# A background of index scores and selection, paced at other rates

## The chip, the cores and the metric

The kernel runs on one core of one Trainium2 chip. A time is device microseconds of one execution; before the change the median of 3 runs is 3255.93 us (3255.27 to 3256.39). TensorE is called PE here, VectorE DVE, ScalarE ACT, GpSimd POOL, and SyncE, which issues most DMAs, SP.

## The reference

One residual block over 2048 rows of width 1024, in float32. What matters here is the indexer of the sparse attention, cut to its core:

```
proj = x @ w_in                       # q, latent, q_idx, w_idx, k_idx, pool_in, gate_logits
# rotary turn of q, k_lat, q_idx, k_idx
for each block of 128 queries:
    rel = relu(einsum('bqhd,bsd->bqhs', q_idx, k_idx) * idx_scale)        # 8 index heads
    score = einsum('bqh,bqhs->bqs', w_idx * head_w_scale, rel)            # inadmissible: -inf
    sel = top_k(score, 256)
    attention over the 256 kept keys (8 heads, shared latent key)
branch_b = multiscale_pool(pool_in) @ w_pool_branch
x = LN(alpha*x + (gate_a*(attn @ w_attn_branch) + gate_b*branch_b) @ w_out)
x = LN(alpha*x + conv_ffn(x))
```

## The kernel before

Every float32 matrix product is done as three products of split operands (`mm3`, line 308: high times high, high times low, low times high). A weight tile is split once, on POOL for the projections (`split`, line 293: a tensor_scalar, then a tensor_tensor that subtracts).

The 2048 rows are worked in four row groups of 512 (`run`, line 1851). First comes the index stage: `proj_index` for the groups 0 to 3 makes the index queries and keys. A second loop then runs `proj_pool`, `proj_q` and `proj_gates` for the groups 0 to 3. In its first round, group 0, the weights are loaded raw, split on POOL and stored; the rounds 1 to 3 load the split parts. Then follow the attention, the output projection and the FFN.

Beside this foreground runs a background: three generators (`GROUPS`, line 65), one for the row groups 0 and 1, one for group 2, one for group 3. Each first makes index scores (`index_scores`, line 879), then selects (`select`, line 946).

- A score step is one index head of one block, or of one half of the keys of a longer block: two or four matmuls, a Relu on ACT, and on DVE a scalar_tensor_tensor (`b<-b,ws,b`) that adds the weighted scores up. It ends in the bare `yield` at line 942. When a block is next in line its query rows are loaded by a DMA on SP (`m<-qi`), doubled on DVE, transposed on PE and split.
- The selection finds for every row the value of its 256th largest score bit by bit, 32 bits. A selection step counts one block against the candidate: DVE counts the front keys (a tensor_scalar that accumulates, `m,cd<-b,F`; the trace calls it TENSOR_SCALAR_CACHE_REDUCE, with a DVE_READ_ACCUMULATOR behind it), ACT the back keys (Sign, `m<-b,F`). After the blocks of a half three small DVE instructions decide the bit (`g<-cd,ca`, `h<-g`, `F<-h,F`); the next count of that half needs F. For the first generator a bit takes six steps (blocks 2, 3 and blocks 4 to 7).
- Then the equal values are counted (`m,c2<-b,F`), and for each block ACT makes signs (`b<-b,tn`), DVE a prefix sum and three more passes, and the mask goes to DRAM over SP.

What sets the order is a planner. `Clocks` and `Paced` (lines 86 to 135) add up an estimated time for each instruction of PE, DVE, ACT and POOL as the program is written. After each step of the foreground `turn` (line 329) adds to a credit the estimated PE time that has passed, times RATE, up to CAP. While credit is left and the estimated backlog of DVE or ACT is below SLACK, it takes the next background step and subtracts the larger of its estimated DVE and ACT time. So RATE is the share of estimated PE time that the background gets.

The attention of row group 3 needs the masks of the blocks 12 to 15. `load_masks` (line 1069) runs whatever is left of the background on the spot, ahead of all later attention work, when the first unit of that group is loaded.

Of the kernel before, what the change touches and what calls it, by code (L numbers as in the profile page):

```python
# [67 lines left out]
NFIRST = 1  # L68
FINE = "fine"
PAUSE = "pause"  # L70
GRAIN = 1
RATE = 0.75
CAP = 1.5
EARLY = 2
SWITCH = "A--"
# [169 lines left out]
class Kern:  # L245
    def __init__(self, ctx, tc, a, out):
        self.ctx = ctx
        self.clocks = Clocks()
        self.tc, self.nc, self.a, self.out = tc, PacedCore(tc.nc, self.clocks), a, out
        self.stores, self.older, self.bg, self.late = [], [], [], []  # L250
        self.const = ctx.enter_context(tc.tile_pool(name="const", bufs=1))
        self.big = ctx.enter_context(tc.tile_pool(name="big", bufs=42))
        self.mid = ctx.enter_context(tc.tile_pool(name="mid", bufs=8))
        self.sm = ctx.enter_context(tc.tile_pool(name="sm", bufs=4))
        self.p1 = ctx.enter_context(tc.tile_pool(name="p1", bufs=4, space=PSUM))
        self.p2 = ctx.enter_context(tc.tile_pool(name="p2", bufs=2, space=PSUM))
        self.early = ExitStack()
        self.keys_pool = self.early.enter_context(tc.tile_pool(name="keys", bufs=1))
        self.dram = ctx.enter_context(tc.tile_pool(name="dram", bufs=1, space=bass.MemoryType.DRAM))
        self.n = 0  # L260
        self.credit = self.seen = 0.0

    def _name(self, s):
        self.n += 1
        return f"{s}{self.n}"
# [63 lines left out]
    def turn(self, step=None):  # L329
        for t in self.late:  # L330
            t[0] -= 1
        while self.late and self.late[0][0] <= 0:
            self.late.pop(0)[1]()
        if step != FINE:
            for dst, src in self.older:
                self.nc.sync.dma_start(dst, src)
            self.older, self.stores = self.stores, []
        pe, work = self.clocks.pe, self.clocks.work
        self.credit = min(self.credit + RATE * (pe - self.seen), CAP)
        self.seen = pe  # L340
        while self.bg and self.clocks.backlog() < SLACK and self.credit > 0:
            ready, gen = self.bg[0]
            if not ready():
                break
            before = dict(work)
            step = next(gen, "end")
            if step == "end":
                self.bg.pop(0)
            if step == PAUSE:
                break  # L350
            self.credit -= max(work["dve"] - before["dve"], work["act"] - before["act"])

    def run_to_end(self, gen):
        for step in gen:
# [163 lines left out]
    def proj_t(self, ps, w, c0, pairs=range(DC // 2)):  # L518

        for dc in (2 * c + i for c in pairs for i in range(2)):  # L520
# [3 lines left out]
            self.mm3(ps, wh[:, j, c0:c0 + P], wl[:, j, c0:c0 + P], xh[:, i], xl[:, i], dc == 0, dc == DC - 1)  # L524
            if i and dc + 1 < DC and (dc // 2) % GRAIN == GRAIN - 1:
                yield FINE
# [352 lines left out]
    def index_scores(self, g):  # L879
        nc = self.nc  # L880
        blocks = [b for b in range(g * RB, (g + 1) * RB) if b >= 2]
        rows, doubled, parts = {}, {}, {}

        def load(b):
            rows[b] = self.M([P, IH * ID])
            nc.sync.dma_start(rows[b], self.d_qi[b])

        def double(b):
            qd = doubled[b] = self.T([P, IH, 2, ID])
            nc.vector.tensor_copy(qd, rows.pop(b).rearrange("p (h d) -> p h d", d=ID)[:, :, None, :]  # L890
                                  .to_broadcast([P, IH, 2, ID]))

        def prepare(b):
            qd = doubled.pop(b)
            ps = self.PS2([P, IH, P])
            for h in range(IH):
                nc.tensor.transpose(ps[:, h], qd[:, h].rearrange("p a d -> p (a d)"), self.ident)
            parts[b] = self.split_new(ps)

        load(blocks[0])  # L900
        for _ in range(PN[0] if g in PG else 1):
            yield PAUSE
        double(blocks[0])
        for _ in range(PN[1] if g in PG else 1):
            yield PAUSE
        prepare(blocks[0])
        for _ in range(PN[2] if g in PG else 1):
            yield PAUSE
        for b in blocks:
            N = P * (b + 1)  # L910
            more = b + 1 in blocks
            if more:
                load(b + 1)
            qh, ql = parts.pop(b)
            if N <= 1024:
                spans = [(0, N)]
            else:
                spans = [(0, N - SPLIT[b // 2]), (N - SPLIT[b // 2], N)]
            tiles = [self.T([P, hi - lo]) for lo, hi in spans]
            self.I[b] = tiles  # L920
            for h in range(IH):
                if h == HD and more:
                    double(b + 1)
                if h == HP and more:
                    prepare(b + 1)
                wsc = self.ws[:, b, h:h + 1]
                for t, (lo, hi) in enumerate(spans):
                    nch = 1 if hi - lo <= 512 else 2
                    cw = (hi - lo) // nch
                    ps = self.PS2([P, 2, 512])  # L930
                    for c in range(nch):
                        ks = slice(lo + c * cw, lo + c * cw + cw)
                        nc.tensor.matmul(ps[:, c, :cw], qh[:, h], self.kst[:, ks], start=True, stop=False)
                        nc.tensor.matmul(ps[:, c, :cw], ql[:, h], self.kst[:, ks], start=False, stop=True)
                    rl = self.T([P, nch, cw])
                    nc.scalar.activation(rl, ps[:, :nch, :cw], AF.Relu, scale=ID ** -0.5)
                    rl = rl.rearrange("p c w -> p (c w)")
                    if h == 0:
                        nc.vector.tensor_scalar(tiles[t], rl, wsc, None, op0=OP.mult)
                    else:  # L940
                        nc.vector.scalar_tensor_tensor(tiles[t], rl, wsc, tiles[t], op0=OP.mult, op1=OP.add)
                    yield
            w = tiles[-1].shape[1]
            getattr(nc, MS).memset(tiles[-1][0:64, w - 64:w], NEG)

# [905 lines left out]
    def run(self):  # L1851
# [23 lines left out]
            done = self.finish_index(g)  # L1875
        self.load_parts(0, range(NFIRST, DC // 2))
        for g in range(NG):
            for i, step in enumerate(self.proj_pool(g)):
                if i == 1 and g == 0:
                    done()  # L1880
                    self.wi_parts = None
                self.turn(step)
            self.run_to_end(self.proj_q(g))
            self.run_to_end(self.proj_gates(g))
# [40 lines left out]
```

## Time and profile before

| | us |
|---|---|
| median of 3 runs | 3255.93 |
| the profiled execution | 3255.52 |
| its span, first to last instruction | 3253.7 |
| PE busy | 3106.2 |
| DVE busy | 2415.8 |
| ACT busy | 1613.8 |
| POOL busy | 642.8 |

The span is 1.8 us short of the execution's own time. PE is busy 95% of it, so 147.5 us are left in which it does nothing. Busy time of PE also grows where its granted clock falls. In this trace the index stage runs to about 218 us, the first row group's projections from 218 to 437 us, those of the groups 1 to 3 to 1082 us, and the attention to 1588 us.

### The profile page before, as it was taken

Reading aid. Unit: us, or ns where it says so; the run is one execution under the profiler, and the core shown is the slowest. Engines: PE = TensorE matmul, PEld = TensorE weight load, DVE = VectorE, ACT = ScalarE, POOL = GpSimd, SP = SyncE. Lnnn points to the kernel's source line nnn. Section 1 sums busy time; section 2 is a strip of 40 time slices with the busy share of each in tenths; the row PEclk is TensorE's granted clock in tenths of the full one; section 3 lists DMA queues with packets and bytes.
Section 4 is the critical chain, followed back from the end, with each engine's and each line's share of the span. In section 5 each row is a group of like instructions: output and inputs, shape, how many; then the busy total and the mean of one; then the engine's idle time right before and its main releaser. Section 6 shows DMA issues by size and latency. Waiting matters only on the chain. (4 is left out here: it accounts for less than half of the span.)

```text
span 3253.7 us, 44390 instructions
## 1 busy us (share of the span) xinstructions
PE 3106.2 (95%) x15014; PEld 2585.8 (79%) x15014; DVE 2415.8 (74%) x4642; ACT 1613.8 (50%) x3068; POOL 642.8 (20%) x592
## 2 busy tenths in 40 slices
PE   8998899999999999699999999999999999999998
PEld 8886688888888787488787877878788887888876
DVE  5589987987799989988766799889855555453465
ACT  3365746874678777577411244444432232442343
POOL 2027410010010211000412244445111111000000
PEclk9999899999999999899999999999999999999999
DMA  7667784754575332211546788788666665653554
GB/s 250 233 203 275 247 329 160 259 213 166 177 265 205 118 105 62 93 59 62 200 143 208 262 281 297 285 298 295 245 213 217 225 228 199 234 197 109 205 222 154
DMA packets 306833, 666.88 MB, mean 205 GB/s; under 512 B 25322, under 2 KB 130222, under 8 KB 306606
## 3 DMA queue, kind: packets, MB, share of 16 engines
q1 hardware_dynamic: 297966, 648.31, 56.6%
q10 hardware_dynamic: 8640, 15.73, 1.3%
q8 instruction: 119, 1.95, 0.2%
q14 instruction: 108, 0.88, 0.1%
HBM read 434.67 MB, written 229.28 MB: 204 GB/s over the span
## 5 line engine op out<-in xcount | busy, mean ns | idle before, releaser
L133 PE MATMUL p<-b,b 128*128 128x512 f32 (+3 forms) x12832 | 2888.3, 381 | 104.6 <-ACT b L133 37.9
L133 PEld LDWEIGHTS p<-b,b 128*128 128x128 f32 x12832 | 2305.6, 190 | 559.4 <-ACT b L133 40.7
L133 ACT ACTIVATE b<-p 128x512 fp32r<-128x512 f32 (+11 forms) x618 | 351.5, 603 | 245.8 <-PE p L133 235.5
L133 DVE TENSOR_TENSOR b<-p,b 128x512 fp32r<-128x512 f32 (+5 forms) x574 | 362.7, 652 | 148.5 <-PE p L133 102.7
L133 ACT ACTIVATE b<-b 128x1024 fp32r<-128x1024 f32 (+2 forms) x310 | 265.8, 874 | 305.3 <-DVE b L133 94.0
L133 ACT ACTIVATE m<-b,F 128x448 bf16<-128x448 f32 (+3 forms) x448 | 366.3, 821 | 87.9 <-DVE F L133 69.3
L133 DVE TENSOR_SCALAR_CACHE_REDUCE m<-b,F 128x512 bf16<-128x512 f32 (+6 forms) x476 | 370.0, 808 | 0.9
L133 DVE TENSOR_TENSOR b<-b,b 128x1024 fp32r<-128x1024 f32 (+4 forms) x224 | 282.9, 1268 | 72.4 <-ACT b L133 48.3
L133 POOL TENSOR_TENSOR b<-b,b 128x1024 f32<-128x1024 f32 (+3 forms) x94 | 231.5, 2464 | 480.5 <-DVE b L133 399.0
L133 DVE SCALAR_TENSOR_TENSOR b<-b,cw,b 128x1022 f32<-128x1022 f32 (+1 forms) x176 | 248.0, 1419 | 94.4 <-ACT b L133 93.5
L133 ACT ACTIVATE b<-m 128x512 fp32r<-128x512 f32 (+1 forms) x248 | 143.9, 587 | 301.0 <-DVE m L133 121.4
L133 ACT ACTIVATE b<-b,cw 128x1024 f32<-128x1024 f32 x88 | 106.8, 1236 | 290.0 <-DVE b L133 290.0
L133 DVE TENSOR_TENSOR b<-m,b 128x512 fp32r<-128x512 f32 (+1 forms) x248 | 163.7, 667 | 86.2 <-ACT b L133 86.0
L133 ACT ACTIVATE b<-b,mx 128x1024 f32<-128x1024 f32 (+2 forms) x192 | 171.7, 896 | 73.9 <-DVE mx L133 71.9
L133 PE MATMUL p<-ident,b 128*128 128x128 f32 x1248 | 194.9, 275 | 9.5 <-DVE b L133 7.3
L133 DVE SCALAR_TENSOR_TENSOR b<-b,ws,b 128x768 f32<-128x768 f32 (+5 forms) x154 | 155.8, 1040 | 49.2 <-ACT b L133 46.6
L133 DVE CUSTOM_DVE_ANT_0 b<-p,b 128x1024 f32<-128x1024 f32 (+2 forms) x192 | 173.5, 906 | 20.5 <-PE p L133 19.7
L133 PEld LDWEIGHTS p<-ident,b 128*128 128x128 f32 x1248 | 152.6, 141 | 43.2 <-DVE b L133 5.5
L133 PE MATMUL p<-kst,b 128*128 128x384 f32 (+3 forms) x656 | 151.0, 361 | 4.8 <-DVE b L133 2.5
L133 DVE SCALAR_TENSOR_TENSOR b<-b,p 128x512 f32<-128x512 f32 x64 | 42.8, 683 | 151.7 <-PE p L133 145.2
L133 ACT ACTIVATE m<-p 128x512 f32<-128x512 f32 (+2 forms) x172 | 100.7, 586 | 74.9 <-PE p L133 69.2
L133 PEld LDWEIGHTS p<-kst,b 128*128 128x128 f32 x656 | 112.8, 191 | 26.3 <-ACT b L133 13.7
(122 smaller groups left out, 1593.0 us busy)
## 6 DMA issues: line engine op xcount, KB each, us to landing
b<-wk SPq DMA_DIRECT2D x339, 512.0 KB
wk<-b SPq DMA_DIRECT2D x211, 512.0 KB
b<-in_w_ffn_down_dram SPq DMA_DIRECT2D x110, 512.0 KB
b<-in_w_ffn_up_dram SPq DMA_DIRECT2D x44, 512.0 KB
h<-b SPq DMA_DIRECT2D x44, 512.0 KB
b<-vv SPq DMA_DIRECT2D x80, 256.0 KB
m<-h SPq DMA_DIRECT2D x66, 256.0 KB
xT<-b SPq DMA_DIRECT2D x32, 512.0 KB
```

The lines of the kernel that those rows point to most:

```text
L133: return f(*args, **kw)
```

## The change

Three numbers and where they are used. A score step now yields LIGHT, and `turn` charges it 0.7 of its estimate. The rate, a constant 0.75 before, is an attribute: 0.75 through the index stage, 0.6 in `proj_pool`, `proj_q` and `proj_gates` of row group 0, and 0.75 from group 1 on. Selection steps are charged as before. No instruction is added or taken away.

```diff
+LIGHT = "light"
 GRAIN = 1
 RATE = 0.75
+RATE_FIRST = 0.6
+SHARE_LIGHT = 0.7
...
         self.credit = self.seen = 0.0
+        self.rate = RATE
...
-        self.credit = min(self.credit + RATE * (pe - self.seen), CAP)
+        self.credit = min(self.credit + self.rate * (pe - self.seen), CAP)
...
-            self.credit -= max(work["dve"] - before["dve"], work["act"] - before["act"])
+            cost = max(work["dve"] - before["dve"], work["act"] - before["act"])
+            self.credit -= cost * SHARE_LIGHT if step == LIGHT else cost
...
-                    yield
+                    yield LIGHT
...
         for g in range(NG):
+            self.rate = RATE if g else RATE_FIRST
             for i, step in enumerate(self.proj_pool(g)):
```

In the order of the instructions lines of the changed file read 3 higher (L136 for L133, the recording helper); the number behind a name is its buffer.

On DVE in the index stage: the third of the four copies of index keys (`kst`), and what stands ahead of it. Before:

```order
L133 TENSOR_SCALAR b_2556<-b_2562,ws_90 128x896
L133 SCALAR_TENSOR_TENSOR b_2556<-b_2577,ws_90,b_2556 128x896
L133 COPY b_2600<-m_2554 128x1024
L133 SCALAR_TENSOR_TENSOR b_2556<-b_2591,ws_90,b_2556 128x896
L133 SCALAR_TENSOR_TENSOR b_2556<-b_2607,ws_90,b_2556 128x896
L133 TENSOR_TENSOR kst<-p_717_2627,m_2640 64x512
```

Now:

```order
L136 TENSOR_SCALAR m_2738,cd_2697<-b_2590,F_2678 128x576
L136 TENSOR_SCALAR m_2751,cd_2748<-b_1850,F_2705 128x128
L136 SCALAR_TENSOR_TENSOR g_2754<-cd_2697,ca_2698 128x4
L136 TENSOR_SCALAR h_2755<-g_2754 128x4
L136 TENSOR_SCALAR m_2765,cd_2748<-b_1928,F_2705 128x256
L136 TENSOR_SCALAR F_2756<-h_2755 128x4
L136 TENSOR_SCALAR m_2779,cd_2776<-b_2039,F_2756 128x192
L136 SCALAR_TENSOR_TENSOR g_2782<-cd_2748,ca_2749 128x2
L136 TENSOR_SCALAR h_2783<-g_2782 128x2
L136 SCALAR_TENSOR_TENSOR F_2784<-h_2783,F_2705 128x2
L136 TENSOR_TENSOR kst<-p_780_2795,m_2808 64x512
```

Before, the scores of block 6 (896 keys) are being added up here; now all scores of the blocks 2 to 7 are done and the selection has begun. Ahead of the third copy stand 37 score rows before and 48 now, with 9 counting rows. Ahead of the fourth copy stand 4 counting rows before and 22 now.

On DVE in the first row group: the first to the fourth eviction of the pooling map (`pscale`), whose matmuls wait for ACT. Before:

```order
L133 SCALAR_TENSOR_TENSOR b_4602<-p_1395_4598,pscale_111,b_4602 128x512
L133 TENSOR_SCALAR m_4611,cd_4608<-b_1850,F_4552 128x128
L133 TENSOR_SCALAR m_4630,cd_4608<-b_1958,F_4552 128x256
L133 SCALAR_TENSOR_TENSOR b_4622<-p_1405_4618,pscale_111,b_4622 128x512
L133 SCALAR_TENSOR_TENSOR g_4648<-cd_4608,ca_4609 128x2
L133 TENSOR_SCALAR m_4645,cd_4642<-b_2262,F_4616 128x192
L133 SCALAR_TENSOR_TENSOR b_4638<-p_1409_4634,pscale_111,b_4638 128x512
L133 TENSOR_SCALAR h_4649<-g_4648 128x2
L133 SCALAR_TENSOR_TENSOR F_4650<-h_4649,F_4552 128x2
L133 TENSOR_SCALAR m_4667,cd_4642<-b_2419,F_4616 128x320
L133 SCALAR_TENSOR_TENSOR b_4656<-p_1418_4652,pscale_111,b_4656 128x512
```

Now:

```order
L136 SCALAR_TENSOR_TENSOR b_4593<-p_1391_4589,pscale_111,b_4593 128x512
L136 SCALAR_TENSOR_TENSOR b_4603<-p_1394_4599,pscale_111,b_4603 128x512
L136 SCALAR_TENSOR_TENSOR b_4619<-p_1398_4615,pscale_111,b_4619 128x512
L136 TENSOR_SCALAR m_4623,cd_4550<-b_2590,F_4536 128x576
L136 SCALAR_TENSOR_TENSOR b_4630<-p_1402_4626,pscale_111,b_4630 128x512
```

Between the first and the fourth eviction stood four counts and the three instructions of a decision; now one count. From the fourth key copy to the fourth of these evictions there are 114 counting rows before and 92 now.

On DVE at the masks that `load_masks` forces, from the last small instruction of blocks 14 and 15 (`tn`) on. Before:

```order
L133 TENSOR_SCALAR tn_15920<-t_15919 128x2
L133 TENSOR_SCALAR b_15891<-b_15890 128x1792
L133 SCALAR_TENSOR_TENSOR b_15892<-b_15891 128x1792
L133 SCALAR_TENSOR_TENSOR nd_15897<-b_15892,fx_15502,cg_15501 128x1
L133 TENSOR_SCALAR nd_15897<-nd_15897 128x1
L133 TENSOR_SCALAR b_15891<-b_15892,nd_15897 128x1792
L133 TENSOR_TENSOR b_15890<-b_15890,b_15891 128x1792
L133 TENSOR_SCALAR b_15902<-b_15890 128x1792
L133 TENSOR_SCALAR b_15932<-b_15931 128x1920
L133 SCALAR_TENSOR_TENSOR b_15933<-b_15932 128x1920
```

Now:

```order
L136 TENSOR_SCALAR tn_15920<-t_15919 128x2
L136 TENSOR_SCALAR b_15932<-b_15931 128x1920
L136 SCALAR_TENSOR_TENSOR b_15933<-b_15932 128x1920
L136 SCALAR_TENSOR_TENSOR nd_15938<-b_15933,fx_15917,cg_15916 128x1
L136 TENSOR_SCALAR nd_15938<-nd_15938 128x1
```

The seven rows of block 13 (1792 keys) are gone from here; they stand some units earlier, between attention work. Block 14 (1920 keys) now follows `tn` directly. Behind the attention's first row maximum stand 15 counting rows before and 6 now; of the last four of them three stood back to back ahead of the small instructions, and now two.

## Rows read from the trace of the kernel before

**Rows 1.** The page's first part: busy us (share of the span) and instructions.

```profile
PE 3106.2 (95%) x15014; PEld 2585.8 (79%) x15014; DVE 2415.8 (74%) x4642; ACT 1613.8 (50%) x3068; POOL 642.8 (20%) x592
```

**Rows 2.** Windows: length, then busy PE, PEld, DVE, ACT, POOL; PEclk, DMA share, GB/s.

```profile
46.00:90.00 44.00, 40.71 (x321) 39.25 (x321) 20.35 (x95) 14.67 (x37) 0.00 (x0) 0.96 0.46 147
90.00:218.00 128.00, 119.21 (x834) 112.15 (x832) 83.52 (x189) 65.95 (x130) 9.16 (x6) 0.96 0.54 184
218.00:250.00 32.00, 27.83 (x131) 21.94 (x129) 26.77 (x89) 18.70 (x55) 14.48 (x13) 1.00 1.03 357
250.00:300.00 50.00, 45.17 (x192) 35.58 (x192) 46.30 (x127) 29.23 (x89) 35.89 (x34) 1.00 0.73 262
300.00:359.00 59.00, 41.39 (x157) 31.05 (x157) 55.92 (x165) 39.54 (x118) 37.11 (x22) 0.86 0.79 283
359.00:437.00 78.00, 78.00 (x337) 64.38 (x337) 73.83 (x259) 54.73 (x169) 32.56 (x24) 0.97 0.80 279
437.00:1082.00 645.00, 644.44 (x2948) 534.32 (x2947) 549.21 (x1253) 433.94 (x776) 49.63 (x68) 1.00 0.59 210
1082.00:1335.00 253.00, 241.60 (x1440) 201.62 (x1438) 228.88 (x632) 190.40 (x429) 48.33 (x64) 1.00 0.29 87
1335.00:1366.00 31.00, 1.62 (x4) 1.02 (x4) 29.81 (x42) 7.32 (x11) 2.80 (x2) 0.57 0.32 109
```

**Rows 3.** Waits of PE from 218 to 360 us: total, times, longest us.

```profile
PE p L133 <- ACT m L133: 12.7, 5, 3.7
PE p L133 <- POOL b L133: 9.6, 9, 2.1
```

**Rows 4.** DVE groups from 218 to 359 us: xcount, busy us, mean ns, idle before.

```profile
L133 DVE SCALAR_TENSOR_TENSOR F<-h,F 128x4 int32<-128x4 int32 x18 | 15.4, 853 | 0.3
L133 DVE TENSOR_SCALAR_CACHE_REDUCE m<-b,F 128x576 bf16<-128x576 f32 x19 | 15.3, 806 | 0.0
...
L133 DVE DVE_READ_ACCUMULATOR m<-b,F 128x1 f32 x112 | 9.1, 81 | 0.0
...
L133 DVE TENSOR_SCALAR_CACHE_REDUCE m<-b,F 128x128 bf16<-128x128 f32 x19 | 6.5, 340 | 0.1
```

**Rows 5.** Timeline of DVE and POOL, 350 to 372 us: start, us, engine, instruction.

```profile
357.00 0.16 DVE L133 SCALAR_TENSOR_TENSOR F<-h,F 128x4 int32<-128x4 int32 x1
...
360.66 2.37 POOL L133 TENSOR_TENSOR b<-b,b 128x1024 fp32r<-128x1024 f32 x1
360.68 2.37 DVE L133 SCALAR_TENSOR_TENSOR F<-h,F 128x2 int32<-128x2 int32 x1
```

**Rows 6.** Timeline of PE, 1310 to 1372 us, with the idle time before in brackets.

```profile
1347.35 0.69 PE L133 MATMUL p<-b,b 128*128 128x384 f32 x1 [12.21 <-ACT b L133]
1365.20 2.90 PE L133 MATMUL p<-b,b 128*128 128x512 f32 x6 [17.16 <-DVE mx L133]
```

**Rows 7.** Timeline of DVE, 1333 to 1372 us.

```profile
1333.69 1.27 DVE L133 TENSOR_SCALAR_CACHE_REDUCE m<-b,F 128x1024 bf16<-128x1024 f32 x1
...
1338.79 0.17 DVE L133 TENSOR_SCALAR tn<-t 128x2 f32<-128x2 f32 x1
...
1346.88 1.19 DVE L133 TENSOR_SCALAR b<-b 128x1792 bf16<-128x1792 f16 x2
...
1363.83 1.22 DVE L133 CUSTOM_DVE_ANT_0 b<-p,b 128x1024 f32<-128x1024 f32 x1
```

**Rows 8.** Timeline of ACT, 1335 to 1348 us.

```profile
1339.07 4.16 ACT L133 ACTIVATE b<-b,tn 128x896 f16<-128x896 f32 x4 [1.95 <-DVE tn L133]
```

**Rows 9.** Waits of PE from 90 to 218 us.

```profile
PE p L133 <- DVE b L133: 4.3, 4, 1.8
PE p L133 <- ACT b L133: 4.3, 5, 1.8
```

**Rows 10.** Window inside the scores of row group 3, columns as in rows 2.

```profile
770.00:886.00 116.00, 115.92 (x533) 95.47 (x532) 80.87 (x87) 68.63 (x82) 0.00 (x0) 1.00 0.36 127
```

## The prediction

> **What bounds the kernel now.** I read the page's first part, then windows by stage, then the waits and DVE's groups where PE stands still. PE is the bound: 3106.2 us of the 3253.7 us span, 95%; DVE is second with 2415.8 us [rows 1]. The change adds no instruction, so PE's work stays, and time can only come from idle time of PE and from matmuls at a low clock. The windows say where these are [rows 2]. From 437 to 1082 us PE is busy 644.44 of 645 us at full clock: nothing to win, much to lose. Up to 1588 us two places stand out.
>
> The first is 250 to 359 us, in row group 0. PE is idle 4.8 and 17.6 us there, and its granted clock is 0.86 in the second window, so for part of it the lower level, 1.2 of 2.4 GHz, behind idle time. DVE is busy 46.30 of 50 and 55.92 of 59 us. At the mean of the quiet stretch (644.44/2948 = 0.219 us) the 192 + 157 matmuls would take 76 us; they took 109. With the 4.2 us idle from 218 to 250 some 37 us are lost from 218 to 359: the ceiling of what can come back there. Directly behind it, 359 to 437 us, the same background runs with DVE at 73.83 of 78 us, and PE is never idle: DVE's density alone does not stall PE. What is special ahead of 359 is that POOL splits the raw weights nearly without a pause (35.89 of 50, 37.11 of 59 us). PE waits 12.7 us for ACT's evictions and 9.6 us for POOL's weights [rows 3]. ACT's evictions stand behind its Sign counts, which need F from DVE, and F is slow: 0.16 us when POOL is quiet, 2.37 us when it starts with a POOL tensor_tensor [rows 5], 853 ns in the mean [rows 4].
>
> The second is 1335 to 1366 us: PE is busy 1.62 of 31 us, and DVE 29.81 [rows 2]. PE waits 12.21 and 17.16 us [rows 6] while DVE works off the forced masks in one piece, from the counts at 1333.69 to the first attention instruction at 1363.83: 30.1 us [rows 7].
>
> **The change part by part.** Only the order moves. Score steps are charged 0.7, so they run up to 1/0.7 = 1.43 times as densely; in row group 0 selection steps run at 0.6/0.75 = 0.8 of their density.
>
> Row group 0. Between the fourth key copy and the pooling map stand 114 counts before and 92 now: 22 steps leave. The trace has 112 steps from 218 to 359 us [rows 4]. What is one worth? Lower end: its own work, the mean of the longest and the shortest of the six counts, (806 + 340)/2 = 573 ns, and one small decision instruction per step at 160 ns [rows 4, 5]: 0.73 us, so 22 x 0.73 = 16. Upper end: all DVE busy time of the stretch charged to the steps, (26.77 + 46.30 + 55.92)/112 = 1.15 us, so 25. PE runs at the pace of that chain here, since its evictions wait in it, so DVE's time comes out of the span until PE is the bound again. I take 18, near the lower end: 9.6 us of PE's waits are on POOL, whose work does not change, though it too waits for DVE at times. If the stretch is not paced by DVE at all the gain is 0; with the whole loss gone it is 37.
>
> The row shows F taking exactly as long as the POOL instruction it meets, 2.37 and 2.37 us [rows 5]. The Trainium skill ("SBUF — State Buffer", section "Who interferes with whom") says why: the port pair that VectorE and GpSimd share is an exclusive lock, and the loser blocks for the whole instruction. By that rule the blocked time is bought by POOL's instructions, which all stay, so a step that leaves saves only its own work: the first row group would give the 16 of the lower end, where the rows' plain DVE share gives 25. The trace agrees on the lock; it does not show how many waits go with the steps.
>
> Attention. Now block 13 is gone from the forced piece, from behind `tn` (1338.79 + 0.17) to its mask. The mask is the first of two at 1346.88 that together took 1.19 us, so the piece ends near 1347.5: 8.5 us. One of three back-to-back counts goes too: 1.2 us. Against that, block 14's prefix sum now follows `tn` directly and must wait for two Signs of ACT, which took 4.16/4 = 1.04 us each [rows 8]; block 13 covered them before. That is 2.1 us of new wait. In all 30.1 - 8.5 - 1.2 + 2.1 = 22.5 us: a gain of 7.6. Bounds: 0 if PE finds another wait at once, 9.7 if the Signs are early. Block 13's chain does not vanish, it stands between units. But nine counts (15 before, 6 now) leave the attention, at up to 1.27 us each [rows 7] some 10 us for the 8.5 that come in, so I cost it at nothing; without that cover it costs up to 8.5, as DVE is busy 228.88 of 253 us there [rows 2].
>
> Index stage. 18 selection steps and up to 11 score steps come in earlier than before. On DVE the 18 are 18 x 0.73 = 13 us, on a DVE that is idle 128 - 83.52 = 44.5 us from 90 to 218; ACT has 62 us free [rows 2]. Their matmuls and query loads only change places; the loads (SP, one per block, DMA share 0.54) pass foreground stores that nothing here waits for. PE is idle 3.3 of 44 us without a background (46 to 90, 7.5%) and 8.8 of 128 with it (6.9%): no price per step is visible. Lower bound 0; upper bound one mean gap of PE there, 8.6/9 = 0.96 us [rows 9], for each of 29 steps: 28. I take 3, by the row that shows no price.
>
> Groups 1 to 3. The score steps run denser and what they free goes to selection earlier. DVE is busy 80.87 of 116 us inside such a stretch [rows 10], 0.70; 1.43 times that is 1.00 at the very most. PE's slack hides it; if DVE were late, the price is the third rival's. Selection keeps its 0.75. I take 1 (0 to 5).
>
> Sum against the profiled execution: 3255.5 - 18 - 7.6 + 3 + 1 = 3233.9. That execution stands 0.4 us below the median of 3255.93, so 3234.
>
> **The rivals.** First: POOL and the raw weights pace row group 0, not DVE. For it: PE's nine waits on POOL, and 78 us with dense DVE and no idle PE. Against it: the longer waits are on ACT, behind F. Then about half of the 12.7 us comes back, 6: 3255.9 - 6 - 7.6 + 4 = 3246.
>
> Second: the stalls feed on each other (idle PE, low clock, late evictions), and the whole loss goes. For it: the clock of 0.86. Against it: DVE would still need (129.0 - 22 x 1.15) = 104 us for what PE could do in some 106. 3255.9 - 37 - 7.6 = 3211.
>
> Third, the slower side: denser score steps make DVE the bound between 437 and 1082 us. 128 of the 176 score steps lie there. If a third of them make PE wait for an eviction, at the 0.96 us of such a gap [rows 9], that is 41 us: 3255.9 - 25.6 + 4 + 41 = 3275. It decides from 6.5 + 25.6 - 4 = 28 us, 0.22 us per step: less only eats the gain up. For it: 0.70 x 1.43 leaves DVE no room, and PE has no slack of its own there. Against it: 0.56 us idle in 645 with DVE at 0.85 already.
>
> Fourth: the steps move, but neither place yields: 3255.9 + 1 to 4 = about 3258.
>
> **How the numbers follow.** Forecast 0.62, its own range 3225 to 3243 by the bounds of the two gains. First rival 0.17, second 0.09, third 0.06, fourth 0.06. The range of 3217 to 3251 leaves out the last two and most of the second. About 0.2%, 6.5 us, is what a measurement of this kernel can tell from no change: faster means below 3249.4. The forecast, the second rival and most of the first (0.13) give 0.84; same gets 0.10 (the rest of the first, most of the fourth), slower 0.06.
>
> **What would show it.** Right: from 218 us to the pooling map PE's waits on ACT well below 12.7 us, PE's clock there near 1, the stretch some 18 us shorter; the standstill before the last row group's attention near 22 us; the index stage as long as before; no idle PE up to attention. Wrong: waits on ACT as long as before, with POOL's waits; idle PE inside a score stretch; or the forced piece ending no sooner.

## The result, and the profile after: slower by 0.5%

The changed kernel takes 3272.98 us (median of 6 runs, 3267.54 to 3276.46) against 3255.76 us for the kernel before, run beside it (6 runs, 3251.54 to 3260.78): ratio 1.0051, 95% interval 1.0037 to 1.0065. The forecast was 3234 us, faster. The profiled execution took 3267.54 us with a span of 3265.8 us, at the low end of the runs; the two spans that are compared here lie 12.1 us apart, the two medians 17.

The page's first part, to be held against [rows 1]: PE's busy time grew by 7.3 us with the same 15014 matmuls, DVE's and ACT's hardly moved.

```profile
PE 3113.5 (95%) x15014; PEld 2589.9 (79%) x15014; DVE 2414.8 (74%) x4642; ACT 1615.3 (49%) x3068; POOL 653.5 (20%) x592
```

The windows by stage, columns as in [rows 2]. The index stage now ends at 230 us instead of 218, row group 0 at 440 instead of 437, the groups 1 to 3 at 1098 instead of 1082.

```profile
90.00:230.00 140.00, 123.17 (x831) 111.70 (x830) 92.73 (x229) 76.26 (x166) 10.22 (x6) 0.96 0.48 160
230.00:266.00 36.00, 28.70 (x130) 23.02 (x129) 24.05 (x99) 17.49 (x51) 14.42 (x13) 0.91 1.02 351
...
313.00:372.00 59.00, 48.67 (x195) 37.73 (x195) 56.95 (x146) 38.84 (x114) 44.34 (x26) 0.88 0.96 335
...
440.00:1098.00 658.00, 649.38 (x2949) 534.77 (x2948) 568.22 (x1332) 442.40 (x797) 55.53 (x77) 1.00 0.56 203
1098.00:1348.00 250.00, 237.36 (x1402) 200.70 (x1401) 219.03 (x580) 183.51 (x412) 48.50 (x59) 0.97 0.30 92
1348.00:1379.00 31.00, 8.13 (x41) 6.22 (x40) 28.09 (x46) 10.13 (x18) 5.43 (x2) 0.68 0.19 69
```

From 90 us to the end of the index stage the same work of PE took 140 us instead of 128 (831 matmuls against 834 in the records). PE is idle 16.8 us there, 8.8 before.

To see where the 12 us come from I cut both traces at the first matmul of each stage. In us, PE's idle time in parentheses (counted from the first matmul to the last). Here and in the expectations below, the pool map that closes the second stage is the projection `proj_pool`, which ends at 250 us before; the pooling map with its evictions (`pscale`) lies in the stage behind it.

| stage | before | after | difference |
|---|---|---|---|
| to 90 us (no background) | 90.0 (5.4) | 89.6 (5.2) | -0.3 |
| rest of index stage, pool map of row group 0 | 160.2 (13.1) | 176.4 (24.2) | +16.2 |
| q and gates of row group 0 | 186.9 (22.3) | 174.1 (12.9) | -12.8 |
| row groups 1 to 3 | 644.9 (0.6) | 657.6 (8.6) | +12.7 |
| attention, 22 units up to the standstill | 236.9 (11.4) | 241.0 (12.6) | +4.0 |
| the unit with the standstill | 48.5 (29.4) | 41.7 (22.9) | -6.9 |
| all the rest | 1873.9 (45.8) | 1873.0 (46.1) | -0.9 |

The differences add up to 12.0. Both forecast gains are there, smaller; three losses outweigh them. Idle time of PE is not all of a difference: of the 16.2 us 11.1 are idle time, of the 12.7 us 8.0, of the 4.0 us 1.2. The rest is the same matmuls taking longer at a lower granted clock, for example 0.91 from 230 to 266 us, against 1.00 from 218 to 250 us in [rows 2]. Here are the rows behind each.

**The index stage.** PE's waits from 90 to 230 us, to be held against [rows 9] (8.6 us in 9 waits, none over 1.8):

```profile
PE p L136 <- ACT b L136: 9.4, 9, 3.0
PE p L136 <- ACT m L136: 3.5, 1, 3.5
PE p L136 <- DVE b L136: 3.3, 5, 1.6
```

The timeline of PE, idle time in brackets, with the three longest waits between 90 and 266 us:

```profile
143.63 1.67 PE L136 MATMUL p<-ident,b 128*128 128x128 f32 x8 [3.49 <-ACT m L136]
...
187.87 1.53 PE L136 MATMUL p<-kst,b 128*128 128x448 f32 x4 [3.04 <-ACT b L136]
...
246.88 12.49 PE L136 MATMUL p<-b,b 128*128 128x512 f32 x48 [6.99 <-DVE kst L136]
```

Each follows a chain. The timeline of ACT shows that ahead of the first two ACT itself stood at a Sign count that waited for DVE's scores:

```profile
142.97 0.51 ACT L136 ACTIVATE m<-b,F 128x256 bf16<-128x256 f32 x1 [2.51 <-DVE b L136]
...
186.26 0.67 ACT L136 ACTIVATE m<-b,F 128x448 bf16<-128x448 f32 x1 [3.26 <-DVE b L136]
```

The second wait is not density alone. POOL splits the first raw weight tile just then, and two of the rotary turns of 16 elements on DVE, 0.17 us each at 143 us with POOL idle, took 2.37 and 1.01 us ahead of that count (timelines of DVE and POOL below). The kernel before meets the same split at 162 us: one such turn took 1.00 us there, and PE waited 1.79 us, the longest of the four waits on DVE in [rows 9].

```profile
181.63 2.37 DVE L136 TENSOR_TENSOR rope<-b,cos 128x16 f32<-128x16 f32 x1
184.01 1.01 DVE L136 TENSOR_TENSOR rope<-b,cos 128x16 f32<-128x16 f32 x1
```

```profile
180.98 2.99 POOL L136 TENSOR_TENSOR b<-b,b 128x1024 fp32r<-128x1024 f32 x1
```

The third is the fourth key copy. The third key copy now comes behind more score rows on DVE, and SP waits for the value splits behind it with four stores (`vv`). So the loads for row group 0 are issued at 225 to 236 us, where before they were at 213 to 223 us, and the stores of the index queries (`qi`) come behind them, from 236.55 us on. The DMA share is high then (1.02 from 230 to 266 us), as it was before (1.03 from 218 to 250 us). The timeline of SP's DMAs, and the activation on ACT that then waits 7.83 us for one of the late stores:

```profile
219.19 5.66 SPq L340 DMA_DIRECT2D vv<-b  x4
224.94 4.71 SPq L520 DMA_DIRECT2D b<-xT  x6
229.74 1.46 SPq L205 DMA_DIRECT2D b<-in_w_in_dram  x2
231.26 5.18 SPq L205 DMA_DIRECT2D b<-in_wq_dram  x2
```

```profile
245.41 0.59 ACT L136 ACTIVATE m<-p 64x512 fp32r<-64x512 f32 x1 [7.83 <-DMA qi<-b]
```

**Row group 0.** PE's waits from 230 to 372 us. Without the key copy they are 13.4 us, 0.9 of it in two short waits not shown; before, the two rows of [rows 3] alone were 22.3. ACT's fell from 12.7 to 8.2 and POOL's from 9.6 to 4.3. The longest on ACT grew from 3.7 to 5.9.

```profile
PE p L136 <- ACT m L136: 8.2, 3, 5.9
PE p L136 <- DVE kst L136: 7.0, 1, 7.0
PE p L136 <- POOL b L136: 4.3, 6, 1.2
```

The counts themselves, from DVE's groups of the same stretch: 96 steps instead of the 112 of [rows 4], and F of the larger half at 703 ns instead of 853 (first row).

```profile
L136 DVE SCALAR_TENSOR_TENSOR F<-h,F 128x4 int32<-128x4 int32 x16 | 11.3, 703 | 0.3
...
L136 DVE DVE_READ_ACCUMULATOR m<-b,F 128x1 f32 x96 | 7.7, 81 | 0.0
```

**Row groups 1 to 3.** The timeline of PE has one long wait that the kernel before has not, in the pooling map of group 1:

```profile
594.59 1.65 PE L136 MATMUL p<-b,wpool 128*128 128x512 f32 x3 [4.83 <-ACT m L136]
```

The timeline of ACT ahead of it: the copy of a gate tile at 587.52, then five Signs of the selection, the last of which waits for F, and only behind them the two evictions that PE needs (its wait ends with the second).

```profile
587.52 0.58 ACT L136 ACTIVATE m<-p 128x512 f32<-128x512 f32 x1
588.06 0.94 ACT L136 ACTIVATE m<-b,F 128x768 bf16<-128x768 f32 x1
...
592.45 0.94 ACT L136 ACTIVATE m<-b,F 128x768 bf16<-128x768 f32 x1 [0.82 <-DVE F L136]
...
593.38 0.67 ACT L136 ACTIVATE b<-p,pscale 128x512 fp32r<-128x512 f32 x1
593.96 0.58 ACT L136 ACTIVATE m<-p 128x512 f32<-128x512 f32 x1
```

**Attention.** The timeline of PE: the two parts of the standstill are 7.47 and 15.40 us, against 12.21 and 17.16 in [rows 6]; ahead of them stand short waits beside the mask of block 13, which now lies between units.

```profile
1313.37 0.50 PE L136 MATMUL p<-b,b 128*128 128x512 f32 x1 [1.61 <-ACT b L136]
1315.96 0.48 PE L136 MATMUL p<-ident,b 128*128 128x128 f32 x1 [2.08 <-DVE b L136]
1318.55 2.92 PE L136 MATMUL p<-b,b 128*128 128x512 f32 x6 [1.37 <-DVE mx L136]
1362.01 0.69 PE L136 MATMUL p<-b,b 128*128 128x384 f32 x1 [7.47 <-ACT b L136]
1378.09 2.92 PE L136 MATMUL p<-b,b 128*128 128x512 f32 x6 [15.40 <-DVE mx L136]
```

### The profile page after: what moved, and what is told of

It reads as the page before. It is cut to its first block, busy times and chain, and to the rows that moved or that the text cites. A ratio compares the mean times of both kernels' runs of the same rounds, so it can differ in the third digit from the quotient of the medians.

```text
span 3265.8 us, 44365 instructions
## 1 busy us (share of the span) xinstructions
PE 3113.5 (95%) x15014; PEld 2589.9 (79%) x15014; DVE 2414.8 (74%) x4642; ACT 1615.3 (49%) x3068; POOL 653.5 (20%) x592
## 5 line engine op out<-in xcount | busy, mean ns | idle before, releaser
L136 PE MATMUL p<-b,b 128*128 128x512 f32 (+4 forms) x12832 | 2887.9, 381 | 102.8 <-ACT b L136 37.5
L136 PEld LDWEIGHTS p<-b,b 128*128 128x128 f32 x12832 | 2308.1, 190 | 554.5 <-ACT b L136 49.4
L136 DVE TENSOR_TENSOR b<-p,b 128x512 fp32r<-128x512 f32 (+5 forms) x574 | 363.5, 652 | 171.3 <-PE p L136 102.8
L136 ACT ACTIVATE b<-p 128x512 fp32r<-128x512 f32 (+11 forms) x618 | 350.9, 603 | 230.9 <-PE p L136 219.8
L136 ACT ACTIVATE b<-b 128x1024 fp32r<-128x1024 f32 (+2 forms) x310 | 266.1, 874 | 305.0 <-DVE b L136 119.3
L136 ACT ACTIVATE m<-b,F 128x448 bf16<-128x448 f32 (+3 forms) x448 | 366.3, 820 | 97.5 <-DVE F L136 74.7
L136 DVE TENSOR_SCALAR_CACHE_REDUCE m<-b,F 128x512 bf16<-128x512 f32 (+6 forms) x476 | 370.9, 808 | 3.9 <-DMA gm<-m 3.3
L136 DVE TENSOR_TENSOR b<-b,b 128x1024 fp32r<-128x1024 f32 (+4 forms) x224 | 285.8, 1281 | 70.6 <-ACT b L136 48.2
L136 POOL TENSOR_TENSOR b<-b,b 128x1024 f32<-128x1024 f32 (+3 forms) x94 | 231.7, 2467 | 480.8 <-DVE b L136 391.1
L136 DVE SCALAR_TENSOR_TENSOR b<-b,cw,b 128x1022 f32<-128x1022 f32 (+1 forms) x176 | 247.8, 1417 | 94.7 <-ACT b L136 93.9
L136 ACT ACTIVATE b<-m 128x512 fp32r<-128x512 f32 (+1 forms) x248 | 143.9, 587 | 305.8 <-DVE m L136 126.3
L136 ACT ACTIVATE b<-b,cw 128x1024 f32<-128x1024 f32 x88 | 106.8, 1236 | 288.8 <-DVE b L136 288.8
L136 DVE TENSOR_TENSOR b<-m,b 128x512 fp32r<-128x512 f32 (+1 forms) x248 | 164.3, 670 | 85.5 <-ACT b L136 85.3
L136 ACT ACTIVATE b<-b,mx 128x1024 f32<-128x1024 f32 (+2 forms) x192 | 171.7, 896 | 82.1 <-DVE mx L136 81.0
L136 PE MATMUL p<-ident,b 128*128 128x128 f32 x1248 | 196.6, 276 | 10.8 <-DVE b L136 5.4
L136 DVE CUSTOM_DVE_ANT_0 b<-p,b 128x1024 f32<-128x1024 f32 (+2 forms) x192 | 173.6, 907 | 22.7 <-PE p L136 21.5
L136 PEld LDWEIGHTS p<-ident,b 128*128 128x128 f32 x1248 | 154.2, 142 | 44.6 <-DVE b L136 7.4
L136 DVE SCALAR_TENSOR_TENSOR b<-b,ws,b 128x768 f32<-128x768 f32 (+5 forms) x154 | 153.1, 1022 | 29.1 <-ACT b L136 26.2
L136 PE MATMUL p<-kst,b 128*128 128x384 f32 (+3 forms) x656 | 150.9, 364 | 8.3 <-ACT b L136 6.0
L136 DVE SCALAR_TENSOR_TENSOR b<-b,p 128x512 f32<-128x512 f32 x64 | 42.8, 683 | 150.7 <-PE p L136 144.3
L136 ACT ACTIVATE m<-p 128x512 f32<-128x512 f32 (+2 forms) x172 | 100.9, 586 | 81.9 <-PE p L136 70.7
L136 PEld LDWEIGHTS p<-kst,b 128*128 128x128 f32 x656 | 110.5, 189 | 37.0 <-ACT b L136 25.1
```

The costliest lines, as they stand in the source:

```text
L136: return f(*args, **kw)
```

## The experiments

Two theories went into them. One: the forecast terms are real and independent, and the loss is that of the dense score steps in the index stage alone. Its rival: wherever background steps are put, they make waits of their own, so that a gain at one place is paid at another. The letters in the expectations are those of each expectation itself.

One table serves all of them. Each column is a stage of the table above, as the difference in us from the first profile of the kernel before; the last two are the ratio of times to the kernel before and its 95% interval.

| run | index + pool map 0 | q, gates 0 | groups 1-3 | 22 units | standstill unit | rest | ratio | interval |
|---|---|---|---|---|---|---|---|---|
| before, second profile | -1.0 | -1.5 | +0.3 | +1.0 | -0.1 | -0.1 | | |
| the change | +16.2 | -12.8 | +12.7 | +4.0 | -6.9 | -0.9 | 1.0051 | 1.0037-1.0065 |
| 1: rate only | -1.5 | -15.4 | +8.0 | -3.3 | +33.8 | -1.5 | 1.0055 | 1.004-1.007 |
| 2: light only | +22.3 | +0.3 | +20.8 | +4.1 | -29.6 | +1.5 | 1.0054 | 1.0039-1.0069 |
| 3: selection held | +15.4 | -9.4 | +13.7 | -3.5 | +11.7 | -3.2 | 1.0076 | 1.006-1.0093 |
| 4: light late | -1.4 | -14.5 | +12.9 | -3.0 | +9.4 | -3.7 | 0.9999 | 0.999-1.0009 |
| 5: light late, rate 0.75 | -0.6 | -0.6 | +12.3 | +10.3 | -17.8 | -1.7 | 1.0007 | 0.9998-1.0016 |
| 6: light late, rate 0.85 later | -1.6 | -13.8 | +39.0 | +10.2 | -29.6 | -2.3 | 0.9992 | 0.9983-1.0001 |
| 7: loads ahead | +18.5 | -14.2 | +14.5 | +4.6 | -6.9 | -0.8 | 1.0046 | 1.0033-1.0058 |
| 8: light early | +18.6 | +1.3 | +19.8 | +7.7 | -8.2 | -1.0 | 1.0104 | 1.009-1.0117 |
| 9: light early, 0.85 | +13.8 | +2.4 | +9.5 | +4.8 | -5.2 | -4.0 | 1.0059 | 1.0045-1.0072 |
| 10: rate by group | +1.9 | -13.0 | +24.0 | +4.6 | -11.4 | -0.9 | 0.9984 | 0.9975-0.9993 |
| 11: 30 bits | +1.3 | 0.0 | +8.9 | -2.3 | -22.0 | -4.5 | 0.9949 | 0.9935-0.9962 |

The stretch up to 90 us, left out, differs by -1.8 to +1.1. The stages are those of one profiled execution, the ratio is one of medians. The profiled execution lies within 2 us of its run's median but for three: the change 5.4 us below it, run 10 8.0 us above it, run 11 5.6 us below it.

**Run 1, the rate alone** (3275.56 us):

```diff
-SHARE_LIGHT = 0.7
+SHARE_LIGHT = 1.0
```

> Only the rate of 0.6 in row group 0; score steps charged in full. The changed kernel lost 12 us in the index stage and 4 at the start of row group 0, and won 13 behind that. Theory A (the denser score steps cause the loss in the index stage) and theory B (the selection steps that come in early there cause it) both expect the index stage as before, to 218 us. Both expect row group 0 up to the pooling map 10 to 13 us shorter. The selection then runs later everywhere: 32 background steps are forced before the last row group's attention (12 before), by the planner's estimate 63 us of DVE against 36, so the standstill of 30 us grows to about 57. Sum: 3255.5 - 12 + 27 = 3270 us. Theory C (any move of background steps costs some us by new collisions) adds 5 to 12 in row groups 1 to 3: 3275 to 3282.

**Run 2, the light steps alone** (3274.68 us):

```diff
-RATE_FIRST = 0.6
+RATE_FIRST = 0.75
```

> Only the charge of 0.7 for score steps; the rate stays 0.75. A and B: the index stage loses the same 12 us as in the changed kernel. Row group 0 keeps its stalls (no gain of 13). No step is left to be forced, so the standstill of 30 us goes, and the masks of all four blocks stand between attention units, where the changed kernel lost 11 us for two. Groups 1 to 3: the changed kernel lost 12 there; theory C says the same again, A says less, since no wait there is bound to the charge. A: 3255.5 + 12 - 30 + 15 + 3 = 3255; C: 3265.

Run 1 gave 15.4 us in row group 0 and lost 33.8 at the standstill: what is not selected there is selected later, and in the end on the spot. The two parts of the standstill are now 46.34 and 17.03 us, in the timeline of PE in run 1:

```profile
1368.90 0.69 PE L136 MATMUL p<-b,b 128*128 128x384 f32 x1 [46.34 <-ACT b L136]
1386.61 2.90 PE L136 MATMUL p<-b,b 128*128 128x512 f32 x6 [17.03 <-DVE mx L136]
```

Run 2 is the mirror image: the standstill goes (29.6 us), row group 0 stays, and the index stage and the groups 1 to 3 lose 43 us. Its timeline of PE has one short wait where the standstill was:

```profile
1384.03 1.68 PE L136 MATMUL p<-b,b 128*128 128x512 f32 x6 [1.56 <-DVE mx L136]
```

So each half of the change moves what it was forecast to move, and each is slower by itself.

**Runs 3 and 4: what lengthens the index stage?** Run 3 is the changed kernel with the selection of the first generator held back until the second loop; only dense score steps are left in the index stage. Run 4 keeps the selection and charges the score steps of the row groups 0 and 1, all of which lie in the index stage, in full.

```diff
 for g in groups:
     yield from self.index_scores(g)
+while self.hold:
+    yield PAUSE
...
 for g in range(NG):
     self.rate = RATE if g else RATE_FIRST
+    self.hold = False
```

> The changed kernel, but the selection of row groups 0 and 1 may not begin before the second loop, so the index stage holds the dense score steps without early selection. A: PE still idles about 17 us from 90 us to the end of the index stage, which ends at 228 to 232 us. B: PE idles about 9 us there as before, and the stage ends at 218 to 221. Behind it the selection is 18 to 22 steps late and 15 steps are forced (44 us by the planner's estimate, 36 before): the standstill is about 37 us. Total by A 3255.5 + 12 - 10 + 7 + 5 = 3270, by B 3257.

```diff
-yield LIGHT
+yield LIGHT if g > 1 else None
```

> The changed kernel, but score steps of row groups 0 and 1 are charged in full; 0.7 only for groups 2 and 3. A and B: index stage as before (218 us), row group 0 to the pooling map 10 to 13 us shorter, 15 steps forced (42 us by estimate), standstill about 36. A: 3255.5 - 12 + 6 + 4 = 3254. C: 5 to 12 more from new collisions in groups 1 to 3 and attention: 3259 to 3266.

Run 3 (3280.39 us) still has 15.4 us of the index loss, run 4 (3257.26 us) none of it. Dense score steps are the cause there, not the selection that starts early. Run 4 also shows what is left without the index loss: 14.5 us won in row group 0, 12.9 lost in the groups 1 to 3, 9.4 at the standstill, no change in all.

**Runs 5 and 6: can the two gains be had together with the index stage left alone?** Both are run 4 with another rate. Run 5 has 0.75 in row group 0 too; run 6 keeps 0.6 there and takes 0.85 in the groups 1 to 3 (and, since the rate is not set again, in the attention), so that no step is left to be forced.

```diff
-RATE_FIRST = 0.6
+RATE_FIRST = 0.75
```

> Score steps are charged 0.7 only for the row groups 2 and 3, and the rate is 0.75 throughout. By the planner's order 3 forced steps are left before the last row group's attention (12 before the change, 15 with the same light steps and the rate 0.6). Theory A (what is saved in row group 0 is paid again as forced work, so without the lower rate neither shows): index stage ends near 218 us and row group 0 near 437 us as before, the standstill at the 22nd attention unit falls from 29 us idle to about 12, time about 3240 us. Rival C (every shift of steps buys a new wait of its own size, here the masks of the blocks 12 and 13 between the units): standstill shorter but the units 16 to 20 some 10 us longer, time 3250 to 3256 us.

```diff
-self.rate = RATE if g else RATE_FIRST
+self.rate = 0.85 if g else RATE_FIRST
```

> Score steps are charged 0.7 only for the row groups 2 and 3; the rate is 0.75 in the index stage, 0.6 in row group 0 and 0.85 in the groups 1 to 3, so that no step is forced in the attention. Theory A (the two gains that were forecast are real and independent of each other once the index stage is left alone): index stage ends near 218 us, row group 0 near 422 us (15 less than before), no standstill (some 25 less), against it 5 to 10 us of mask work between units or of waits in groups 1 to 3: about 3225 us. Rival C (DVE has no room for more background between 437 and 1082 us; stalls there eat it): groups 1 to 3 longer by 15 to 25 us, time 3238 to 3248 us.

Run 5 took 3258.2 us, run 6 3254.12 us. Theory A of both fell: the stages it named did what it said (standstill -17.8 and -29.6, row group 0 as before and -13.8), but the loss came back elsewhere, in run 6 by 39.0 us in the groups 1 to 3 and 10.2 in the attention. The windows of run 6, columns as in [rows 2], show DVE at 125.26 of 137 us in the last part of group 3, from ahead of its pooling map to the attention, PE idle for 15.7 us and its clock at 0.93. Before, this part took 115 us, with DVE busy for 109.53 and PE for 114.56. The longest of the waits there stands in the timeline of PE below; behind it are the timelines of ACT and of SP.

```profile
420.00:967.00 547.00, 536.25 (x2436) 442.28 (x2435) 478.58 (x1105) 367.11 (x671) 39.92 (x60) 0.99 0.56 200
967.00:1104.00 137.00, 121.34 (x513) 98.65 (x512) 125.26 (x315) 90.39 (x165) 12.13 (x15) 0.93 0.50 180
```

```profile
1091.84 11.02 PE L136 MATMUL p<-b,b 128*128 128x128 f32 x42 [8.05 <-ACT b L136]
```

```profile
1091.15 0.63 ACT L136 ACTIVATE b<-m 128x512 fp32r<-128x512 f32 x1 [12.17 <-DMA m<-q]
```

```profile
1076.97 0.32 SPq L340 DMA_DIRECT2D msk<-b  x1
...
1086.93 1.35 SPq L1097 DMA_DIRECT2D m<-q  x2
```

So at 0.85 DVE has 15.7 us more to do in this part, but its share fell, from 0.95 to 0.91: that DVE is full is not what PE waits for here. ACT waits for the queries of the attention, whose loads (`m<-q`) SP issues at 1086.93 us. They stand behind the store of a mask (`msk<-b`), ahead of which SP waited 12.0 us for DVE. Before, they were issued from 1068.04 us on, and no mask was made in this part.

**Run 7: are the late loads the cause in the index stage?** The changed kernel with the six loads of row group 0's x parts issued ahead of the value stores.

```diff
+if c == 1 and g + 1 == NG:
+    self.load_parts(0, range(NFIRST, DC // 2))
 if c == 1 and done:
     done()
...
-self.load_parts(0, range(NFIRST, DC // 2))
```

> The changed kernel, with the six loads of the first row group's x parts issued on SP ahead of the value stores that wait for the third key copy, instead of behind them. Theory A (the index stage is later because the late third key copy holds SP, so that loads and stores then come all at once and the kT store's buffer waits for them): the 7 us wait of PE on the fourth key copy goes, pool map of row group 0 starts 5 to 8 us earlier, time about 3266 us. Theory B (the score steps ahead of the evictions on DVE and ACT cost it directly, the loads are only late beside them): index stage and pool map of row group 0 as long as with the change, 3271 to 3275 us.

3271.03 us; theory B. The 6.99 us wait on the key copy is gone, and PE waits elsewhere instead. The waits of PE in run 7 from 90 to 270 us have no key copy any more, but a longer single wait on ACT and three on DVE's `m`; the stage took +18.5 us, not less than the change's +16.2. PE's idle time in it fell by only 2.1 us (24.2 to 22.1), and its matmuls took 4.3 us longer than with the change, at a mean granted clock of 0.93 instead of 0.95.

```profile
PE p L136 <- ACT b L136: 11.2, 10, 4.5
PE p L136 <- ACT m L136: 3.5, 1, 3.5
PE p L136 <- DVE m L136: 3.5, 3, 1.6
PE p L136 <- DVE b L136: 3.3, 5, 1.6
```

**Runs 8 and 9: the light steps of the index stage alone, at 0.7 and at 0.85** (rate 0.75 throughout).

```diff
-RATE_FIRST = 0.6
+RATE_FIRST = 0.75
...
-yield LIGHT
+yield LIGHT if g < 2 else None
```

> Only the score steps of the row groups 0 and 1, which all run in the index stage, are charged 0.7; the others in full, and the rate is 0.75 throughout. By the planner's order 32 of them now stand in the index stage's third quarter instead of 19. Theory A (dense score steps cost the index stage and the first pool map 14 to 20 us, and nothing gives it back): pool map of row group 0 ends near 267 us (250 before), row group 0's stalls stay as before, 6 forced steps instead of 12 take some 9 us from the standstill: about 3263 us. Rival B (what the index stage loses is background done early, so the later stages give all of it back): 3256 us or less.

> As the run beside it, but the score steps of the row groups 0 and 1 are charged 0.85: 25 of them stand in the third quarter of the index stage (19 before, 32 at 0.7). Theory A (the loss goes with the density of score steps): index stage with the first pool map about 6 to 10 us longer than before, half of what 0.7 costs; 8 forced steps instead of 12: about 3257 to 3259 us. Rival (any change of order there costs the same, since it is a collision and not a density): 14 to 18 us longer, about 3264 us.

Run 8 took 3292.47 us, run 9 3277.05 us, beside 3260.19 us for the kernel before. The index term came as expected in run 8 (+18.6); in run 9 it is +13.8, three quarters of it and not half, so it does not go with the density alone. Both expectations of the time were too low, because they left out the groups 1 to 3: +19.8 and +9.5. One wait of these in run 8 can be read: in the timeline of PE, PE waits for a load of the x parts of group 1.

```profile
468.80 0.80 PE L136 MATMUL p<-b,b 128*128 128x512 f32 x1 [4.78 <-DMA b<-xT]
```

The timeline of SP in run 8 shows why the load is late. A mask of the background is stored ahead of it, and SP waited 14.5 us for DVE before that store:

```profile
446.19 0.32 SPq L340 DMA_DIRECT2D msk<-b  x1
...
457.10 5.13 SPq L520 DMA_DIRECT2D b<-xT  x4
```

The loads go out 0.5 us ahead of the stage (457.6 us). Before, they went out at 431.63 us, 5.5 us ahead of it, and the first mask store came behind them, at 439.31 us. Run 2 has the same wait, 4.83 us, behind a mask store at 448.30 us.

**Run 10: a rate for each group.** Run 4 with 0.6 in row group 0, 0.85 in the groups 1 and 2, 0.75 in group 3.

```diff
-self.rate = RATE if g else RATE_FIRST
+self.rate = 0.85 if g in (1,2) else 0.75 if g else 0.6
```

> Score steps are charged 0.7 only for the row groups 2 and 3; the rate is 0.6 in row group 0, 0.85 in the groups 1 and 2, and 0.75 in the index stage and in group 3. 6 steps are left to be forced. Theory A (the gains can be kept if group 3, where the rate 0.85 throughout bought 15.7 us of idle time, runs at 0.75 again): row group 0 ends near 422 us, groups 1 to 3 take 660 us as with the light steps late, standstill near 42 us with 22 idle: 3255.9 - 15 - 8 + 3 = about 3236 us. Rival C (the background's work on DVE is the same in all orders and finds its price elsewhere): row group 0 shorter by 15, but the groups 1 to 3 or the attention's units longer by about as much, 3250 to 3256 us.

3252.03 us beside 3260.19 us for the kernel before, ratio 0.9984: the best of the orders tried, faster than both kernels by its interval, yet by less than the 0.2% that the prediction takes for a change. Rival C: 13.0 us won in row group 0, 11.4 at the standstill, 24.0 given back in the groups 1 to 3. These are of the execution of 3259.99 us; run 10's executions go from 3249.68 to 3262.68 us, so how the stages of a fast one look is not known.

**Run 11: less work instead of another order.** The kernel before, but its selection decides only 30 of the 32 bits.

```diff
-for bit in range(31, -1, -1):
+for bit in range(31, 1, -1):
```

> The kernel before with its own pacing, but the selection decides 30 of the 32 bits (the threshold's two lowest bits are left out), so that 28 counting steps, 14 of them ahead of the second generator's end, leave the background; one step is left to be forced instead of 12. Theory A (in all orders tried the background's work on DVE finds its price somewhere; less of it gives the standstill back without a new wait): the standstill falls from 29 us idle to 5 or less, the other stages stay within a few us, time about 3256 - 25 = 3231 us. Rival C (the waits come from the place where steps fall and not from their sum, so moving everything behind the first generator by six to twelve steps buys new waits): standstill gone, but 10 to 20 us more in the index-free stages or between the attention's units, 3240 to 3250 us.

3241.14 us beside 3258.39 us for the kernel before, ratio 0.9949. The standstill unit gives 22.0 us back. The timeline of PE in run 11 has this wait where the standstill was (the other one is 0.42 us):

```profile
1335.52 2.71 PE L133 MATMUL p<-b,b 128*128 128x512 f32 x6 [4.26 <-DVE b L133]
```

But even here the groups 1 to 3 lose 8.9 us, although the background as a whole has less to do. That is between the two theories and nearer to C: the place where the steps fall has a price of its own.

**The kernel before, a second time.**

> The kernel before, unchanged, profiled a second time, to see how far the lengths of its stages scatter from one execution to another. Theory A (the order of the instructions sets the waits): every stage as in the first profile within 2 us, the groups 1 to 3 again at 645 us with PE idle under 2 us. Rival (the waits are chance, and the first profile was a lucky one): the groups 1 to 3 up to 10 us longer with several us of idle PE, or the index stage off by more than 5 us.

Theory A: all stages within 1.5 us of the first profile, the groups 1 to 3 at 645.2 us with 0.9 us idle. For this order the waits come again from one execution to the next, and the differences of ten and more in the table are far above what the two profiles differ by. No other order was profiled twice.

## Why the prediction was wrong, point by point

The sum put the stages at -21.6 us, and the profiled execution came out at +12.0. Of these 33.6 us 13.2 are the index stage, 11.7 the groups 1 to 3, 5.2 row group 0 and 4.7 the attention up to the standstill; the rest gave 1.2 back.

- **The index stage was the mis-sized term: +3 forecast, +16.2 measured** (inside the stated bounds of 0 to 28). The step that failed is "no price per step is visible". It compared the idle share of a stretch without a background with that of one order with it, and took the answer for the price of adding steps. The five runs with light steps there and the change itself lost 13.8 to 22.3 us; all the others differed by -1.6 to +1.9. Averages had hidden where the steps stand: DVE and ACT had room over 128 us, but ACT stood 2.51 and 3.26 us at a count while PE's evictions queued behind it. Which single wait carries the loss is not settled: run 7 removed the longest, and the loss stayed, partly as matmuls at a lower clock.
- **The row groups 1 to 3: +1 (0 to 5) forecast, +12.7 measured.** Outside the bounds. "PE's slack hides it" read 0.56 us of idle time in 645 as proof of room. It was the property of that one order: every other order tried lost 8.0 to 39.0 us there, also run 1, which charges no step less, and run 11, which has fewer steps. What makes these waits was read in three places only: 4.83 us behind five Signs on ACT, and 4.78 us in run 8 and 8.05 us in run 6 for loads that stood on SP behind a mask store waiting for DVE. The first is no single case: the change and the runs 2, 4, 5, 6, 7, 8 and 10 all have a wait of 2.1 to 5.8 us at the pooling map of group 1, ended by ACT or DVE. A rule for these waits stays open.
- **Row group 0: the gain came where it was forecast, 12.8 instead of 18, and only in part by the mechanism.** The rate of 0.6 gave 12.8 to 15.4 us in six of the seven runs that have it (9.4 in run 3, whose selection starts late there), and with 0.75 this stage differed by -1.5 to +2.4 us. Over the 22 steps that left, 12.8 us are 0.58 us each, a little below the lower end of 0.73 that the prediction built from a step's own work. PE's waits on ACT fell by 4.5 us, as forecast, but those on POOL by 5.3 us, from 9.6 to 4.3, with POOL's work unchanged (busy 105.5 and 105.4 us in this stage). That speaks against the first rival (POOL paces it), and also against the prediction's reason for taking less than the upper end. One sign did not come: PE's clock, forecast near 1, is 0.88 from 313 to 372 us, where it was 0.86.
- The lock of the Trainium skill ("SBUF — State Buffer", section "Who interferes with whom") would have put this term at 16 instead of 18, nearer to what came. The trace of the changed kernel agrees with the lock: F takes 2.26 us when it comes right behind the start of a POOL tensor_tensor of 2.41 us, in the timelines of DVE and POOL:

```profile
368.77 2.26 DVE L136 SCALAR_TENSOR_TENSOR F<-h,F 128x2 int32<-128x2 int32 x1
```

```profile
368.60 2.41 POOL L136 TENSOR_TENSOR b<-b,b 128x1024 fp32r<-128x1024 f32 x1
```

- **The standstill: right, but not free.** 7.6 forecast, 6.9 measured; the new wait of block 14 on its Signs was put at 2.1 us and DVE waits 2.21 us there (its timeline, the row below). The step "I cost it at nothing" failed: the 22 units before, among which block 13's mask now stands, took 4.0 us longer, 1.2 of it idle time and the rest matmuls at a clock of 0.97 instead of 1.00. The runs 1, 3 and 4 make block 12's mask at the standstill too, which the kernel before has between units, and are 3.0 to 3.5 us shorter there.

```profile
1359.54 0.66 DVE L136 TENSOR_SCALAR b<-b 128x1920 f16<-128x1920 f16 x1 [2.21 <-ACT b L136]
```

- **The idea under all of this failed.** The prediction priced each place by itself. Run 1 shows that time taken out of row group 0 is paid at the standstill unless the background is ahead, and run 2 that the light steps, which put it ahead, pay for that in the index stage and in the groups 1 to 3.
- The second rival's sum leaves out the 4 us for the index stage and the groups 1 to 3 that the others carry: 3215 instead of 3211. The third rival (3275 us, chance 0.06) had the sign and the size, by luck. Its mechanism was another: it put 41 us on score steps between 437 and 1082 us. There were 12.7, and the one long wait lay among selection counts.

## What to carry to other kernels

A stretch in which the bounding engine never idles beside a dense background is proof of a good order, not of room: price a move of background steps by what stands behind them in each in-order queue, not by the busy share of the engines. SP is one of these queues: a background store that waits there holds back the loads behind it (12.0 us in run 6, 14.5 us in run 8). Before a local stall is counted as gain, ask when the same work must be done at the latest, and what it will wait beside then. In ten reordered kernels gains of 13 to 30 us at one place came to 0.2% at best in the whole, while 28 counting steps less gave 0.5%.

## What the runs showed that was not expected

The two profiles of the kernel before agree stage by stage within 1.5 us over 3253 us, down to a standstill of 29.4 and 29.3 us of idle PE. So a wait of several us in a profile belongs to the order and can be followed, although it could not be forecast from the queues' averages. The whole time is less steady: run 10's eleven executions lie up to 13.0 us apart, so a ratio is not read from one profile.

The light steps of the index stage cost run 8 more behind the index stage (19.8 us in the groups 1 to 3) than in it (18.6 us), although the steps that were moved are all done by 210 us and the groups 1 to 3 run from 458 to 1122 us.
